# adaLN vectors of a two-layer diffusion backbone: the first partial sums are added on TensorE, block biases come one turn later, and layer 0's gate-2 blocks move to the output projection

## The chip, the cores and the metric

The kernel runs on one core of one Trainium2 chip. The metric is the device time of one execution in microseconds. Three runs of the kernel before took 2369.32 to 2370.25 us, their median is 2369.73 us.

## The reference

The program computes two layers of a diffusion backbone over 1024 latent tokens of 1024 features, in float32. Layer 0 mixes tokens by differential attention (8 heads, 256 context tokens in front of the latent ones), layer 1 by multi-scale centred pooling. Each layer ends in a dense SwiGLU FFN of width 2816. Every sub-layer is modulated by adaLN vectors and followed by a LayerNorm of `ALPHA * x + gate * y`. Cut to what matters here:

```python
def adaln_params(cond, w_mod, b_mod):
    m = jax.nn.silu(cond) @ w_mod + b_mod          # (1024,) @ (1024, 6144)
    return jnp.split(m, N_MOD, axis=-1)

for i in range(DEPTH):
    sh1, sc1, g1, sh2, sc2, g2 = adaln_params(c[:, None, :], w_mod[i], b_mod[i])
    csh1, csc1, cg1, csh2, csc2, cg2 = adaln_params(c_ctx, w_mod[i], b_mod[i])
    hx = modulate(x, sh1, sc1)                     # h * (1 + scale) + shift
    hc = modulate(h_ctx, csh1, csc1)
    y_lat = (attention of hx and hc) if i == 0 else multiscale_pool(hx, ...)
    x = layer_norm(ALPHA * x + g1 * y_lat, ln_g[i, 0], ln_b[i, 0])
    x = layer_norm(ALPHA * x + g2 * swiglu(modulate(x, sh2, sc2), ffn_w_in[i], ffn_w_out[i]),
                   ln_g[i, 1], ln_b[i, 1])
```

The adaLN vectors of a layer have 6144 entries: six vectors of 1024 features. The kernel makes them in blocks of 512 entries, so a layer has twelve blocks; blocks 0 to 3 are shift 1 and scale 1, and blocks 10 and 11 are gate 2. The context needs blocks 0 to 3 of layer 0 with its own condition.

## The kernel before, in words

**How a block is made.** An adaLN block is a product of a vector with a 1024 x 512 part of `w_mod`. It is done on VectorE: for each of eight row tiles of 128, a `[128, 512]` weight tile is multiplied with the condition's value of its partition and added to an accumulator `gacc` (L320 and L322 in the projections, L112 and L114 in `gemv_half`). Then TensorE adds up the 128 partitions: four matmuls with a matrix of ones on the other side write a PSUM tile `pg` (L298, L117; in float32, so the trace has two records for each matmul). Last, VectorE adds the bias (L299, L118). The weights come in four loads `gw` of 512 KB each.

**The first feature tiles.** Shift 1 and scale 1 of layer 0 are needed first, feature tile by feature tile, and have a layout of their own: `modulate_latents(k)` loads 1 MB (`wm`), makes two partial sums for the even and the odd row tiles (L233, L235; `acc[:, 0]` and `acc[:, 1]`), adds them (L237), sums over partitions on TensorE (`pm`, L240), adds the bias (L242, L243), and modulates the tile: ScalarE scales and rounds (L214, L215), GpSimd makes the low half (L216). TensorE's matmuls of the first three q and k products follow two tiles behind (L262).

**The products.** All large products are split into high and low halves (`fp32r`), so each is three matmuls. For each weight, ScalarE casts the high half and VectorE subtracts for the low half (L136 or L139 and L54 or L141 in the projections, L362 and L363 later).

**Turns.** During the projections, `turn()` is called once after each chain of 24 matmuls in `project_qk`, and before each in `project_v`. A turn takes one of the `turns` entries (a block's `gw` load, two row tiles), so a block takes four turns; the turn after that runs `sum_rows`: `pg` on TensorE and the bias. The first four blocks use the context's condition; when the fourth is summed, `context()` modulates the context tokens. `steps` gives the order of the products: the rest of q group 0, q groups 1 to 3, v group 0, k group 0's context tokens, k groups 1 to 3, v group 1. The loads of the next step's weights are written ahead of each step, through two raw buffers `wr`. There are two accumulators `gacc` and four `gw` buffers in this stage.

**Output projection and FFN.** `gemv1(b)` makes a block of layer 1. Blocks 0 and 1 are made in the output projection, behind feature tiles 1 and 4, and blocks 2 to 11 in layer 0's FFN, one behind each of its first ten groups. A group (of eleven) is: the products of w_in for two halves of 128 hidden features, done with seven products in place of eight (`p0` to `p6`, L641 to L643, 168 matmuls a group), then `beside(g)`, then the products with w_out (96 matmuls). In this stage the `gw` loads, the w_in loads (L693) and the w_out loads (L776) all share the four slots of one tag, `raw`, and there is one accumulator `gacc`.

**Order.** The compile step puts the instructions of each engine, and of each queue that issues DMAs, in a fixed order beforehand: an instruction that is ready by its own estimate goes, and among several ready ones the one that stands first in the program. The engines then run their lists in that order and wait with semaphores. A buffer that is used again waits for the readers of what it held.

Of the kernel before, what the change touches and what calls it, by code (L numbers as in the profile page):

```python
# [14 lines left out]
ALU = mybir.AluOpType  # L15
# [4 lines left out]
P = 128  # L20
D = 1024
KT = D // P
# [16 lines left out]
RAW, AOP, CT, QD = 4, 3, 5, 4  # L39
# [4 lines left out]
def backbone(ctx: ExitStack, tc: tile.TileContext, a: dict, out: bass.AP):  # L44
    nc = tc.nc
    V, S, G, PE, SP = nc.vector, nc.scalar, nc.gpsimd, nc.tensor, nc.sync
# [3 lines left out]
    def ctile(shape, name, dt=F32):  # L50
        return const.tile(shape, dt, name=name, tag=name)
# [9 lines left out]
    ones_f = ctile([P, P], "ones_f")  # L61
# [16 lines left out]
    def small_loads(pool):  # L78
        lamv = pool.tile([P, 4, HD], F32, name="lamv", tag="lamv")
        SP.dma_start(lng, a["lng"])  # L80
        SP.dma_start(lnb, a["lnb"])
        SP.dma_start(subg, a["subg"])
        SP.dma_start(pscale, a["pscale"])
        SP.dma_start(lamv, a["lam"].partition_broadcast(P))
        prod = pool.tile([P, 2, HD], F32, name="lamprod", tag="lamprod")
        V.tensor_tensor(prod[:, 0, :], lamv[:, 0, :], lamv[:, 1, :], ALU.mult)
        V.tensor_tensor(prod[:, 1, :], lamv[:, 2, :], lamv[:, 3, :], ALU.mult)
        ls = ctile([P, 2], "lamsum")
        V.reduce_sum(ls, prod, axis=AX.X)
        le = ctile([P, 2], "lamexp")  # L90
        S.activation(le, ls, AF.Exp)

        V.scalar_tensor_tensor(neglam, le[:, 1:2], -LAM_INIT, le[:, 0:1], ALU.add, ALU.subtract)
# [8 lines left out]
    def gemv_half(pool, psum, pstag, l, b, tags, bufs, wpool):  # L102

        acc = pool.tile([P, 512], F32, name="gacc", tag=tags[0], bufs=bufs[0])
        for k2 in range(KT // 2):
            wt = wpool.tile([P, 2, 512], F32, name="gw", tag=tags[1], bufs=bufs[1])
            SP.dma_start(wt, a["w_mod"][l, k2 * 2 * P:(k2 + 1) * 2 * P, b * 512:(b + 1) * 512]
                         .rearrange("(k p) f -> p k f", p=P))
            for i in range(2):
                k = 2 * k2 + i  # L110
                if k == 0:
                    V.tensor_scalar(acc, wt[:, i, :], sc_sb[:, 0, 0:1], None, ALU.mult)  # L112
                else:
                    V.scalar_tensor_tensor(acc, wt[:, i, :], sc_sb[:, k, 0:1], acc, ALU.mult, ALU.add)  # L114
        pg = psum.tile([P, 4, P], F32, name="pg", tag=pstag)
        for i in range(4):
            PE.matmul(pg[:, i, :], lhsT=acc[:, i * P:(i + 1) * P], rhs=ones_f, start=True, stop=True)  # L117
        V.tensor_tensor(modv[l][:, b * 4:(b + 1) * 4], pg[:, :, 0], bmod[:, l, b * 4:(b + 1) * 4], ALU.add)  # L118
# [4 lines left out]
    with ExitStack() as actx:  # L123
# [89 lines left out]
        def modulated(k, xk, sc, sh, t0, n):  # L213
            S.activation(xk, xk, AF.Identity, scale=sc, bias=sh)  # L214
            S.copy(hT_hi[:, k, t0:t0 + n], xk)  # L215
            G.tensor_tensor(hT_lo[:, k, t0:t0 + n], xk, hT_hi[:, k, t0:t0 + n].bitcast(F32), ALU.subtract)  # L216
# [5 lines left out]

        def modulate_latents(k):
            wm = pe.tile([P, KT, 256], F32, name="wm", tag="ot", bufs=2)
            SP.dma_start(wm, a["w_mod0"][k])
            xk = pa.tile([P, T], F32, name="xk", tag="xk", bufs=2)
            SP.dma_start(xk, a["xT"][k * P:(k + 1) * P, :])
            if k == 0:
                SP.dma_start(bmod, a["bmod"])
            acc = pa.tile([P, 2, 256], F32, name="acc", tag="gacc", bufs=2)  # L230
            for i in range(KT):
                if i < 2:
                    V.tensor_scalar(acc[:, i, :], wm[:, i, :], sc_sb[:, i, 0:1], None, ALU.mult)  # L233
                else:
                    V.scalar_tensor_tensor(acc[:, i % 2, :], wm[:, i, :], sc_sb[:, i, 0:1], acc[:, i % 2, :],  # L235
                                           ALU.mult, ALU.add)
            V.tensor_tensor(acc[:, 0, :], acc[:, 0, :], acc[:, 1, :], ALU.add)  # L237
            pm = psA.tile([P, 2, P], F32, name="pm", tag="mm")
            for i in range(2):
                PE.matmul(pm[:, i, :], lhsT=acc[:, 0, i * P:(i + 1) * P], rhs=ones_f, start=True, stop=True)  # L240
            sh, sc = modv[0][:, k:k + 1], modv[0][:, 8 + k:9 + k]
            V.tensor_tensor(sh, pm[:, 0, 0:1], bmod[:, 0, k:k + 1], ALU.add)  # L242
            V.scalar_tensor_tensor(sc, pm[:, 1, 0:1], 1.0, bmod[:, 0, 8 + k:9 + k], ALU.add, ALU.add)  # L243
            modulated(k, xk, sc, sh, CTX, T)
# [21 lines left out]
        cx = []  # L266

        def load_context():
            for k2 in range(2):
                cx.append(pa.tile([P, 4, CTX], F32, name="xk", tag="xk", bufs=2))  # L270
                SP.dma_start(cx[-1], a["ctxT"][k2 * 512:(k2 + 1) * 512, :].rearrange("(k p) t -> p k t", p=P))

        def context():
            V.tensor_scalar(modx[:, 8:16], modx[:, 8:16], 1.0, None, ALU.add)
            for k2 in range(2):
                xk = cx[k2]
                for k in range(4 * k2, 4 * k2 + 4):
                    modulated(k, xk[:, k % 4, :], modx[:, 8 + k:9 + k], modx[:, k:k + 1], 0, CTX)
# [1 line left out]


        GWL = 3
        turns = [(b, k2, 1) for b in range(4) for k2 in range(4)] + [(b, k2, 0) for b in range(4, 12) for k2 in range(4)]
        loaded, todo = [], []

        def load_rows():
            if len(loaded) < len(turns):
# [5 lines left out]
        def sum_rows():  # L293

            acc, b, j = todo.pop()
            pg = psA.tile([P, 4, P], F32, name="pg", tag="mm")
            for i in range(4):
                PE.matmul(pg[:, i, :], lhsT=acc[:, i * P:(i + 1) * P], rhs=ones_f, start=True, stop=True)  # L298
            V.tensor_tensor((modx if j else modv[0])[:, b * 4:(b + 1) * 4], pg[:, :, 0], bmod[:, 0, b * 4:(b + 1) * 4], ALU.add)  # L299

        done = [0]
        accs = [None]

        def turn():
            if todo:
                sum_rows()
                if done[0] == 12:
                    load_context()
                if done[0] == 16:
                    context()  # L310
            if done[0] == len(turns):
                return
            b, k2, j = turns[done[0]]
            load_rows()
            wt = loaded[done[0]]
            for i in range(2):
                k = 2 * k2 + i
                if k == 0:
                    accs[0] = pa.tile([P, 512], F32, name="gacc", tag="gacc", bufs=2)
                    V.tensor_scalar(accs[0], wt[:, i, :], sc_sb[:, 0, j:j + 1], None, ALU.mult)  # L320
                else:
                    V.scalar_tensor_tensor(accs[0], wt[:, i, :], sc_sb[:, k, j:j + 1], accs[0], ALU.mult, ALU.add)  # L322
            if k2 == 3:
                todo.append((accs[0], b, j))
            done[0] += 1
# [10 lines left out]
        for si, (kind, g, spans) in enumerate(steps):  # L336
            nxt = None
            if si + 1 < len(steps):
                nxt = w1 if si == 0 else weights(*steps[si + 1][0:2])
            if si == 1:  # L340
                small_loads(pa)
            if kind == 2:
                project_v(g, w)
            else:
                project_qk(kind, g, spans, w)
            w = nxt
# [9 lines left out]
    pwt = ctx.enter_context(tc.tile_pool(name="pwt", bufs=1, reuse_waits="tile"))  # L356
# [23 lines left out]
    with ExitStack() as bctx:  # L380
# [90 lines left out]
        for h in range(NH):  # L471
            g, hl = h // 2, h % 2
# [28 lines left out]
    pf = ctx.enter_context(tc.tile_pool(name="pf", bufs=1, reuse_waits="tile"))  # L501
    psM = ctx.enter_context(tc.tile_pool(name="psM", bufs=4, space=PSUM, reuse_waits="tile"))
    psL = ctx.enter_context(tc.tile_pool(name="psL", bufs=4, space=PSUM, reuse_waits="tile"))
# [131 lines left out]
    def gate_vector(l, gi, name):  # L635
        gt = ctile([P, KT], name)
        V.tensor_scalar(gt, modv[l][:, gi * 8:gi * 8 + 8], 1.0 / ALPHA, None, ALU.mult)
        return gt
# [11 lines left out]
        SP.dma_start(zT[:, k, :], a["xT"][k * P:(k + 1) * P, :])  # L650
    g1 = gate_vector(0, 2, "g1_0")
    M0 = ffn_mod(0)
    g2 = gate_vector(0, 5, "g2_0")
    def w_o(d, t0, n):
        wr = wo_raw.pop(0) if wo_raw else raw_o(d)
        p_ = bank()
# [6 lines left out]
        accumulate(d, slice(t0, t0 + n), p_[:, 0:n], g1)  # L663

    H = []
    def gemv1(b):
        gemv_half(pf, psL, "ln", 1, b, ("gacc", "raw"), (1, RAW), wpool=pwt)

    for d in range(KT):
        w_o(d, 0, 512)  # L670
        if d in (1, 4):
            gemv1(d // 4)
    rows = rows_of(0, 4)
    for d in range(KT):
        w_o(d, 512, 256)
# [183 lines left out]
            if t < 6:  # L859
                ln_rows(t, xr[t // 4][:, t % 4, :])  # L860

    ffn(0, g2, 0, M0, H, beside=lambda g: gemv1(g + 2) if g < 10 else None, after=ln_to_pool)

    A1 = one_plus(1, 1, "A1")
    V.tensor_tensor(A1, A1, lng[:, 1, :], ALU.mult)
# [52 lines left out]
    H = []  # L918
# [112 lines left out]
```

## Time and profile before

| | |
|---|---|
| median of 3 runs | 2369.73 us |
| the profiled execution | 2367.97 us, span 2366.2 us |
| TensorE busy | 2251.8 us, 95% of the span |
| VectorE busy | 1695.7 us, 72% |
| ScalarE, GpSimd busy | 932.7 us, 617.3 us |
| TensorE's granted clock over the span | 0.985 |

The page gives busy times of one execution. Matmuls are pipelined, so their records overlap: a matmul of 0.39 us starts every 0.23 us. An idle stretch stands in brackets behind the instruction that it precedes, with what ended it. The span has these stages: first feature tiles to 62 us, projections to 375 us, attention to 760 us, output projection to about 881 us, layer 0's FFN to about 1571 us, pooling, and layer 1's FFN to the end.

### The profile page before, as it was taken

The page shows a single profiled execution, that of the slowest core. Times are in us where ns is not written, and L with a number is a line of the kernel's source. Part 1 is how long each engine was busy: PE and PEld are TensorE (multiplying, and loading weights), DVE is VectorE, ACT ScalarE, POOL GpSimd, SP SyncE. Part 2 cuts the span into 40 slices and gives each one's busy share as a digit, 9 for nine tenths or more (in the row PEclk, how much of TensorE's full clock was granted, in tenths as well). Part 3 has the DMA queues.
Part 4 walks back from the last instruction along what each step waited for, and adds up shares of the span by engine and source line. Part 5 has one row for each costly group of instructions (what it writes and reads, how often), then busy time and mean ns, then how long its engine had stood idle before and what let it go on. Part 6 is the DMA issues. An engine that isn't in the chain of part 4 may idle for free.

```text
span 2366.2 us, 31051 instructions
## 1 busy us (share of the span) xinstructions
PE 2251.8 (95%) x11800; PEld 1916.2 (81%) x11800; DVE 1695.7 (72%) x2580; ACT 932.7 (39%) x1635; POOL 617.3 (26%) x618
## 2 busy tenths in 40 slices
PE   4979998999999997999999999998799999999997
PEld 3868887999998885888888888897588888888886
DVE  7763625999996689777777777757966666666678
ACT  3213115888876354222222222447422222222242
POOL 3432312444443043111111111103411111111122
PEclk9999999999999998999999999999899999999999
DMA  7866746333221532222222222212111111111121
GB/s 265 285 212 194 244 133 169 104 87 88 70 70 48 196 105 81 89 90 89 89 89 81 89 89 89 75 32 83 36 54 54 50 49 53 54 54 51 49 89 72
DMA packets 100918, 236.64 MB, mean 100 GB/s; under 512 B 9376, under 2 KB 27424, under 8 KB 99616
## 3 DMA queue, kind: packets, MB, share of 16 engines
q1 hardware_dynamic: 78688, 210.53, 27.5%
q10 hardware_dynamic: 22080, 24.12, 3.6%
q8 instruction: 93, 1.52, 0.3%
q14 instruction: 57, 0.47, 0.1%
HBM read 206.30 MB, written 28.31 MB: 99 GB/s over the span
## 4 chain that ended last, share of the span: by engine, by line
PE 84%; DVE 11%; DMA 1%; ACT 1%; issue 1%; POOL 1%; SPq 0%; DVEq 0%; ACTq 0%; POOLq 0%
PE mm L643 18%; PE mm L642 18%; PE mm L641 18%; PE s L400 6%; PE misc L431 6%; PE misc L424 3%; PE mm L171 2%; PE mm L170 2%; PE mm L169 2%; PE mm L160 1%; PE mm L161 1%; PE mm L159 1%; DVE aop L363 1%; DVE zT L646 1%; DVE acc L235 1%
## 5 line engine op out<-in xcount | busy, mean ns | idle before, releaser
L641 PE MATMUL mm<-H,aop 128*128 128x512 f32 x1232 | 484.1, 393 | 18.0 <-ACT aop L362 10.5
L643 PE MATMUL mm<-H,aop 128*128 128x512 f32 x1232 | 482.3, 392 | 6.7 <-DVE aop L363 6.7
L362 ACT CAST aop<-raw 128x512 fp32r<-128x512 f32 x392 | 241.8, 621 | 620.8 <-PE mm L643 578.5
L642 PE MATMUL mm<-H,aop 128*128 128x512 f32 x1232 | 483.2, 392 | 3.3 <-DVE H L363 3.3
L646 DVE SCALAR_TENSOR_TENSOR zT<-mm,g,zT 128x512 f32<-128x512 f32 (+1 forms) x400 | 276.9, 704 | 123.1 <-PE mm L643 121.1
L363 DVE TENSOR_TENSOR aop<-raw,aop 128x512 fp32r<-128x512 f32 x392 | 279.5, 716 | 111.3 <-ACT aop L362 110.2
L641 PEld LDWEIGHTS mm<-H,aop 128*128 128x128 f32 x1232 | 233.1, 189 | 68.8 <-ACT aop L362 13.2
L643 PEld LDWEIGHTS mm<-H,aop 128*128 128x128 f32 x1232 | 233.0, 189 | 57.6 <-DVE aop L363 9.6
L642 PEld LDWEIGHTS mm<-H,aop 128*128 128x128 f32 x1232 | 233.3, 189 | 52.3 <-DVE H L363 4.5
L642 PE MATMUL mm<-quad,aop 128*128 128x512 f32 x608 | 237.7, 391 | 1.5 <-DVE quad L363 1.5
L641 PE MATMUL mm<-quad,aop 128*128 128x512 f32 x608 | 237.6, 391 | 0.2 <-ACT aop L362 0.2
L643 PE MATMUL mm<-quad,aop 128*128 128x512 f32 x608 | 236.4, 390 | 0.0
L403 DVE TENSOR_REDUCE mx<-s 128x1 f32<-128x1280 f32 x128 | 190.7, 1490 | 38.7 <-PE s L400 33.8
L400 PE MATMUL s<-kk,qd 128*128 128x512 f32 (+1 forms) x768 | 181.9, 372 | 5.9 <-ACT e L406 3.1
L406 ACT ACTIVATE e<-s,mx 128x1280 f32<-128x1280 f32 x128 | 170.0, 1328 | 24.4 <-DVE mx L403 24.3
L718 POOL TENSOR_TENSOR raw<-s,raw 128x512 f32<-128x512 f32 x40 | 51.9, 1298 | 454.4 <-DVE aop L363 324.5
L400 PEld LDWEIGHTS s<-kk,qd 128*128 128x128 f32 x768 | 135.8, 190 | 30.4 <-ACT e L406 4.2
L431 PE MATMUL misc<-vv,at 128*128 128x128 f32 x1280 | 153.5, 275 | 0.6 <-ACT at L425 0.6
L409 POOL TENSOR_SCALAR e<-e,sm 128x1280 f32<-128x1280 f32 x64 | 88.2, 1378 | 250.7 <-DVE sm L407 247.4
L431 PEld LDWEIGHTS misc<-vv,at 128*128 128x128 f32 x1280 | 148.0, 192 | 0.8 <-ACT at L425 0.8
L642 PEld LDWEIGHTS mm<-quad,aop 128*128 128x128 f32 x608 | 114.2, 188 | 28.5 <-DVE quad L363 5.3
L641 PEld LDWEIGHTS mm<-quad,aop 128*128 128x128 f32 x608 | 114.2, 188 | 24.4 <-ACT aop L362 0.9
(176 smaller groups left out, 4081.3 us busy)
## 6 DMA issues: line engine op xcount, KB each, us to landing
gw<-in_w_mod SPq DMA_DIRECT2D x96, 512.0 KB, 4.5
raw<-in_w_in SPq DMA_DIRECT2D x88, 512.0 KB, 3.6
raw<-in_w_out SPq DMA_DIRECT2D x48, 512.0 KB, 3.4
qd<-q_d SPq DMA_DIRECT2D x64, 256.0 KB, 6.5
raw<-in_w_o SPq DMA_DIRECT2D x24, 512.0 KB, 3.7
kk<-k_d SPq DMA_DIRECT2D x8, 1280.0 KB, 6.3
wr<-in_w_qk SPq DMA_DIRECT2D x18, 512.0 KB, 5.5
wm<-in_w_mod SPq DMA_DIRECT2D x8, 1024.0 KB, 7.3
```

Of the source, the lines that this page charges most:

```text
L362: S.copy(hi, src)
L363: (eng or V).tensor_tensor(lo, src, hi.bitcast(F32), ALU.subtract)
L400: PE.matmul(ps[:, lo_:hi_], lhsT=self.qd[:, m, s, q0:q0 + P], rhs=self.kk[:, m, lo_:hi_], start=(s == 0), stop=(s == 1))
L403: V.tensor_reduce(mx, ps[:, 0:TA], axis=AX.X, op=ALU.max, negate=True)
L406: S.activation(e, ps[:, 0:TA], AF.Exp, bias=mx, accum_out=sm)
L409: G.tensor_scalar(e, e, sm, 1.0, ALU.mult, ALU.mult)
L424: PE.transpose(pt[:, j, :], self.e[0][:, (kb + j) * P:(kb + j + 1) * P], ident)
L431: PE.matmul(av, lhsT=self.at[:, kb, :], rhs=self.vv[:, kb, :], start=(kb == 0), stop=(kb == NTT - 1))
L641: PE.matmul(p_, lhsT=wh, rhs=xh, start=first, stop=False)
L642: PE.matmul(p_, lhsT=wh, rhs=xl, start=False, stop=False)
L643: PE.matmul(p_, lhsT=wl, rhs=xh, start=False, stop=last)
L646: V.scalar_tensor_tensor(zT[:, d, cs], p_, gate[:, d:d + 1], zT[:, d, cs], ALU.mult, ALU.add)
```

## The change

The first `wm` load is issued in four parts. The two partial sums of a first feature tile are no longer added on VectorE: TensorE runs two matmuls for each half of `pm` and adds the partials in PSUM. In the projections, `sum_rows` only issues `pg`, and the bias is added by a new function `vector()` at the next turn, which also starts `context()`. Two turns are left empty at the beginning of step 3 (q group 3), and the list of turns ends with block 9 rather than 11. Blocks 10 and 11 of layer 0 are made in the output projection, where blocks 0 and 1 of layer 1 were made, and the gate-2 vector is built behind them. The twelve blocks of layer 1 are all made in layer 0's FFN: none behind group 0, two behind each of groups 1, 2 and 3, and one behind each of groups 4 to 9.

```diff
         def modulate_latents(k):
             wm = pe.tile([P, KT, 256], F32, name="wm", tag="ot", bufs=2)
-            SP.dma_start(wm, a["w_mod0"][k])
+            if k == 0:
+                for i in range(0, KT, 2):
+                    SP.dma_start(wm[:, i:i + 2], a["w_mod0"][k, :, i:i + 2])
+            else:
+                SP.dma_start(wm, a["w_mod0"][k])
...
-            V.tensor_tensor(acc[:, 0, :], acc[:, 0, :], acc[:, 1, :], ALU.add)
             pm = psA.tile([P, 2, P], F32, name="pm", tag="mm")
             for i in range(2):
-                PE.matmul(pm[:, i, :], lhsT=acc[:, 0, i * P:(i + 1) * P], rhs=ones_f, start=True, stop=True)
+                for j in range(2):
+                    PE.matmul(pm[:, i, :], lhsT=acc[:, j, i * P:(i + 1) * P], rhs=ones_f, start=(j == 0), stop=(j == 1))
...
-        turns = [(b, k2, 1) for b in range(4) for k2 in range(4)] + [(b, k2, 0) for b in range(4, 12) for k2 in range(4)]
-        loaded, todo = [], []
+        turns = [(b, k2, 1) for b in range(4) for k2 in range(4)] + [(b, k2, 0) for b in range(4, 10) for k2 in range(4)]
+        loaded, todo, summed = [], [], []
...
                 PE.matmul(pg[:, i, :], lhsT=acc[:, i * P:(i + 1) * P], rhs=ones_f, start=True, stop=True)
+            summed.append((pg, b, j))
+
+        def vector():
+
+            pg, b, j = summed.pop()
             V.tensor_tensor((modx if j else modv[0])[:, b * 4:(b + 1) * 4], pg[:, :, 0], bmod[:, 0, b * 4:(b + 1) * 4], ALU.add)
+            if j and b == 3:
+                context()
...
+        quiet = [0]
+
         def turn():
+            if quiet[0]:
+                quiet[0] -= 1
+                return
+            if summed:
+                vector()
             if todo:
                 sum_rows()
-                if done[0] == 12:
-                    load_context()
-                if done[0] == 16:
-                    context()
+            if done[0] == 12 and not cx:
+                load_context()
...
             if si == 1:
                 small_loads(pa)
+
+            if si == 3:
+                quiet[0] = 2
...
     M0 = ffn_mod(0)
-    g2 = gate_vector(0, 5, "g2_0")
...
-    def gemv1(b):
-        gemv_half(pf, psL, "ln", 1, b, ("gacc", "raw"), (1, RAW), wpool=pwt)
+    def gemv(l, b):
+        gemv_half(pf, psL, "ln", l, b, ("gacc", "raw"), (1, RAW), wpool=pwt)

     for d in range(KT):
         w_o(d, 0, 512)
         if d in (1, 4):
-            gemv1(d // 4)
+            gemv(0, 10 + d // 4)
+    g2 = gate_vector(0, 5, "g2_0")
...
-    ffn(0, g2, 0, M0, H, beside=lambda g: gemv1(g + 2) if g < 10 else None, after=ln_to_pool)
+    def beside(g):
+        for b in {0: (), 1: (0, 1), 2: (2, 3), 3: (4, 5)}.get(g, (g + 2,) if g < 10 else ()):
+            gemv(1, b)
+
+    ffn(0, g2, 0, M0, H, beside=beside, after=ln_to_pool)
```

## Rows read from the trace of the kernel before

**Rows 1.** The page, part 1: busy time, share of the span, instructions.
```profile
PE 2251.8 (95%) x11800; PEld 1916.2 (81%) x11800; DVE 1695.7 (72%) x2580; ACT 932.7 (39%) x1635; POOL 617.3 (26%) x618
```
**Rows 2.** TensorE's waits, 27 to 380 us: total us, times, longest.
```profile
PE mm L160 <- DVE wl L54: 8.0, 1, 8.0
PE pm L240 <- DVE acc L237: 7.4, 5, 1.5
PE mm L171 <- DVE wl L141: 3.3, 1, 3.3
...
PE mm L159 <- DVE modx L299: 1.7, 1, 1.7
```
**Rows 3.** Stretches: length, busy PE, PEld, DVE, ACT, POOL; PEclk, DMA, GB/s.
```profile
62.00:122.00 60.00, 60.00 (x271) 49.83 (x270) 40.27 (x55) 14.55 (x19) 30.48 (x21) 1.00 0.80 265
...
173.00:176.50 3.50, 3.43 (x9) 2.71 (x10) 3.50 (x5) 0.00 (x0) 1.28 (x1) 0.54 0.78 263
...
996.40:1057.15 60.75, 60.75 (x275) 50.46 (x274) 45.06 (x68) 16.97 (x29) 11.64 (x9) 1.00 0.27 87
```
**Rows 4.** Timeline of TensorE, 173 to 177 us: start, us, what, idle before.
```profile
173.07 0.80 PE L160 MATMUL mm<-wl,hT_hi 128*128 128x512 f32 x1 [7.98 <-DVE wl L54]
...
176.22 0.39 PE L159 MATMUL mm<-wh,hT_hi 128*128 128x512 f32 x1
```
**Rows 5.** Timeline of the first feature tiles, 7 to 24 us.
```profile
7.15 2.46 DVE L235 SCALAR_TENSOR_TENSOR acc<-wm,sc_sb,acc 128x256 f32<-128x256 f32 x6
...
10.12 1.22 PE L240 MATMUL pm<-ones_f,acc 128*128 128x128 f32 x4 [10.12 <-DVE acc L237]
...
20.11 4.55 DVE L235 SCALAR_TENSOR_TENSOR acc<-wm,sc_sb,acc 128x256 f32<-128x256 f32 x6
...
20.96 2.62 POOL L216 TENSOR_TENSOR hT_lo<-xk,hT_hi 128x1024 fp32r<-128x1024 f32 x1 [4.25 <-ACT hT_hi L215]
```
**Rows 6.** Timeline of VectorE at the sum of tile 5's partials.
```profile
45.29 2.48 DVE L237 TENSOR_TENSOR acc<-acc 128x256 f32<-128x256 f32 x1
```
**Rows 7.** L216, 38 to 66 us: ns min/median/max, first and last start.
```profile
L216 POOL TENSOR_TENSOR hT_lo<-xk,hT_hi x5: 2397/2638/2640, 38.4 to 64.4; 128x1024 fp32r<-128x1024 f32 x5
```
**Rows 8.** Timeline of VectorE in the projections.
```profile
122.88 0.16 DVE L299 TENSOR_TENSOR modx<-pg,bmod 128x4 f32<-128x4 f32 x1 [8.10 <-PE pg L298]
122.96 0.48 DVE L320 TENSOR_SCALAR gacc<-gw,sc_sb 128x512 f32<-128x512 f32 x1
...
150.64 0.16 DVE L299 TENSOR_TENSOR modx<-pg,bmod 128x4 f32<-128x4 f32 x1 [11.51 <-PE pg L298]
```
**Rows 9.** TensorE's waits in layer 0's FFN, 935 to 1490 us.
```profile
PE pg L117 <- DVE gacc L114: 1.0, 1, 1.0
```
**Rows 10.** SyncE's queue, 930 to 1490 us: its waits for w_out's slots.
```profile
SPq L776 <- DVE gacc L114: 53.6, 19, 3.1
```
**Rows 11.** Timeline of FFN group 1: w_out loads, pg, first output matmul, bias.
```profile
978.71 3.90 SPq L776 DMA_DIRECT2D raw<-in_w_out  x2
...
995.57 1.05 PE L117 MATMUL pg<-ones_f,gacc 128*128 128x128 f32 x8
996.37 0.48 PE L641 MATMUL mm<-quad,aop 128*128 128x512 f32 x1
...
997.71 0.15 DVE L118 TENSOR_TENSOR modv<-pg,bmod 128x4 f32<-128x4 f32 x1
```
**Rows 12.** The w_out loads (L776), 930 to 1490 us: issue to landing.
```profile
DMA to landing us min/median/max: 3.2/3.5/4.3
```
**Rows 13.** Timeline of VectorE in the output projection, second block.
```profile
783.33 0.49 DVE L112 TENSOR_SCALAR gacc<-gw,sc_sb 128x512 f32<-128x512 f32 x1
...
785.61 4.74 DVE L114 SCALAR_TENSOR_TENSOR gacc<-gw,sc_sb,gacc 128x512 f32<-128x512 f32 x6 [0.24 <-DMA gw<-in_w_mod]
...
790.72 0.69 DVE L363 TENSOR_TENSOR aop<-raw,aop 128x512 fp32r<-128x512 f32 x1 [0.36 <-ACT aop L362]
```
**Rows 14.** Timeline of ScalarE at the context tokens' casts.
```profile
208.98 0.71 ACT L215 CAST hT_hi<-xk 128x256 fp32r<-128x256 f32 x2 [16.21 <-issue]
```

## Prediction

> **What bounds the kernel now.** I read the page first: TensorE is busy for 95% of the span [rows 1], so time is lost or won where TensorE stands idle. Its waits, asked for by stretch, come next. Between 27 and 380 us four of them lie where the change works [rows 2]: five waits for the sum of the two adaLN partials (L237), 7.4 us in all, then 3.3, 1.7 and 8.0 us in the projections, where a weight's low half (L141, L54) or a block's bias (L299) is late on VectorE. From 62 to 122 us and in the FFN groups of layer 0 TensorE has no gap [rows 3]: there, a new wait on TensorE is a loss of its full length. A matmul of 512 columns takes 0.228 us (the 60 us less 16 bias records of 0.11, over 255), a chain of 24 takes 5.5.
>
> A wait also costs clock. After the 8.0 us wait the granted clock over 173 to 176.5 was 0.54, so mostly the 1.2 GHz level [rows 3], and seven matmuls took from 173.07 to 176.22 [rows 4], 3.15 us for 1.6 of work. I add 1.6 us to every wait of 3 us or more and nothing to shorter ones, which is a choice.
>
> **The first feature tiles (L225 to L243).** The first wm load comes in four parts. Today the eight sums start when the whole tile has landed. With parts, six of them lie under the load, four L235 and two L233, at 0.4 and 0.3 each [rows 5] 2.2 us; I take 1.9, as the parts cost issue time. The sum L237 (0.43) goes; pm takes eight records in place of four, which at the spacing there (four in 1.22 [rows 5]) adds 1.2. So the first bias is about 1.1 earlier. It doesn't last: VectorE operations with both inputs in SBUF don't run while GpSimd's L216 runs. Six L235 took 2.46 us alone and 4.55 beside L216 [rows 5]; L237 took 2.48 beside it [rows 6]. Ending sooner, tile 0's L216 falls on the last sums of tile 1, and tile 1's bias is back near its old time.
>
> For tiles 3 to 7 one period is 6.5 us (five L216 from 38.4 to 64.4 [rows 7]), of which 2.9 is VectorE's sums and 2.6 L216 with L237 stuck behind it. Without L237 the sums of one tile slip through before L216 starts (a period of about 4.5), and those of the next begin behind it and are cut by the following one (about 7.4). The mean is 5.9, and over these tiles the last pm comes about 2.1 us sooner. Five pm of four more records cost 2.3 us of TensorE, which lie in what is left of its idle time. TensorE will also have fewer matmuls behind it when the last pm comes, so I take 1.5 us won, between 0 and 4.
>
> The Trainium skill, on its page "SBUF — State Buffer", section "Who interferes with whom", says that a VectorE instruction with two SBUF inputs and a GpSimd instruction that reads SBUF exclude each other, and that whichever issues first holds the port to its end. By that rule the trace agrees, and removing one blocked instruction hands the block to the next; without such a lock all five waits would go, 7.4 less 2.3, so 5.1 us.
>
> **The bias one turn later (L299).** In VectorE's order L299 is followed at once by L320 of the block after next [rows 8], which needs the accumulator that the same pg matmuls free (there are two buffers). VectorE would wait for pg at that place with or without the bias. I take 0, within 2 us either way.
>
> **The two quiet turns and the shorter list.** Two turns are skipped at the start of the fourth q step, so block 2's pg stands two chains (11 us) later, and with it L299, L320 and seven sums. Today VectorE sits 11.51 us before L299 at 150.64 [rows 8], with the first v weight's low half queued behind, and the chain of weight buffers (two raw ones) then delivers the later halves at 173, the wait of 8.0 for L54 [rows 2]. Without it they can be made from about 146 on, and the fourth by 158, before TensorE needs it near 160. So 1.7 + 8.0 + 1.6 of clock, 11.3 us, can go; I take 9.8, as something of it will come back. The wait of 3.3 (and 1.6 of clock) stands behind block 1's pg, ahead of the quiet turns; I leave it. Ends: 0, and 16.2 (all three). The eight turns that leave hide under TensorE now; their leaving is worth 0.
>
> **Gate-2 blocks in the output projection.** gemv(0, 10) and gemv(0, 11) take the places of gemv1(0) and gemv1(1): same loads (eight of 512 KB on SyncE's queue), same sums, same pg. 0.
>
> **The FFN of layer 0.** Group 0 loses its block and the 1.0 us wait for it [rows 9]: −1.0. Groups 1, 2, 3 get two blocks each instead of one, and this is the costly part. One block fits today: its loads take raw slots early, its pg runs at its program place, behind the 168 product matmuls, and w_out is there by then. But every w_out load waits for a slot that the block's sums free (L776 for L114, 19 times) [rows 10]. With two blocks, the second's four gw loads take all four raw slots ahead of w_out, since the queue keeps the program's order; and they can't be used up, since there is one accumulator, which is free only after the first block's pg, at the end of the products. So behind pg stands, in series: the bias from 997.71 to 997.87, L112 and L114 (0.49, and 0.79 as six of them in 4.74 [rows 11, 13], so 1.3), the w_out load, 3.5 us to landing [rows 12], and ScalarE's cast, 0.6. The first output matmul, today at 996.37 [rows 11], would start at 1003.3.
>
> The third matmul also needs VectorE's low half. In the output projection, where two blocks already follow each other, that L363 ran at 790.72, after the last of the second block's sums [rows 13]. Here: eight sums, 6.0 us from 997.87, to 1003.9; L363 0.7, to 1004.6; and up to 1.8 for product results that VectorE still owes. That is 8.2 to 10.0 after 996.37; two matmuls (0.45) and the second pg (0.9) run in the hole, so 6.9 to 8.7 are lost, and 1.6 of clock: 8.5 to 10.3. I take 9.5; the ends are 6.5 (L363 goes first) and 12 (another load ahead in the queue). Three groups: +28.5, between 19.5 and 36. Nothing hides it: TensorE is busy for 60.75 of 60.75 us in a group [rows 3], and the next group's products need raw slots that come after w_out.
>
> **Sum.** −1.5 + 0 − 9.8 + 0 − 1.0 + 28.5 = +16.2 us. The profiled execution took 2367.97 (span 2366.2): 2384.2 for it, and the median of the runs, 2369.73, lies 1.8 above, so 2386. This forecast's own range is 2373 to 2399.
>
> **Rivals.** (1) The w_out wait doesn't appear: the first block's pg slips in among the products (its last sums were done by 982.6, when the second w_out load was issued, 13 us before pg [rows 11]), the second block is summed under the products, and w_out lands in time. It decides if TensorE meets pg some 10 us before the products end. Against it: today's pg stands exactly behind them in every group from 1 on, and only group 0's ever waited [rows 9, 11]. Then the gains alone stand: 2369.7 − 12.3 = 2357, faster. (2) The FFN waits come and the projections win nothing: the context tokens' modulation begins three turns later, and ScalarE stood 16.21 us in front of its casts today [rows 14]. Such a wait in front of the first context chain eats the 9.8, and up to 8 more: 2396 to 2404, middle 2399. That the bias move does nothing is in the sum already.
>
> **Chances.** Forecast 0.61, rival 1 0.22, rival 2 0.17. A measurement tells 0.2%, 4.7 us, from no change. Faster by more: most of rival 1 and a sliver of the forecast, 0.24. Within: 0.08. Slower: 0.68. The range runs from rival 1 to rival 2, 2357 to 2401.
>
> **What would show it.** Right: in groups 1 to 3 a wait of 6 to 9 us on TensorE at its first output matmuls, for L362 or L363 of w_out, with the L776 load issued 1 to 4 us after pg, and a granted clock near half behind it; pm waits of mixed length in place of five of 1.5; no wait of 8 us near 170. Wrong: pg of the first block among the products; groups of 61.6 us; or new waits before the context chain near 200 us.

## The result and the profile after

The changed kernel takes 2389.48 us (median of 5 runs, 2388.46 to 2392.0), the kernel before 2369.73 (5 runs beside it). The ratio is 1.0086, 95% interval 1.0071 to 1.0101, so 17 to 24 us slower. The forecast was 2386, slower, with the doubled FFN groups as the cause. The profiled execution has a span of 2387.7 us.

TensorE's busy time rose by 14 us against [rows 1] (page, part 1). Some 6 of them belong to `pm`, which has 32 records more; and the granted clock over the span fell from 0.985 to 0.981. So part of the loss is clock, not waiting.

```profile
PE 2265.8 (95%) x11832; PEld 1928.1 (81%) x11832; DVE 1688.2 (71%) x2572; ACT 933.1 (39%) x1635; POOL 616.1 (26%) x618
```

Where the time went is read from the same landmarks in both traces, in us from the span's start (first matmul of attention, first w_in product, first w_out matmul of groups 0, 1 and 4, end):

| | attention | FFN | group 0 | group 1 | group 4 | end |
|---|---|---|---|---|---|---|
| before | 375.1 | 874.2 | 933.3 | 996.4 | 1178.6 | 2366.2 |
| changed | 367.9 | 865.7 | 925.0 | 992.5 | 1200.0 | 2387.7 |
| difference | -7.2 | -8.5 | -8.3 | -3.9 | +21.4 | +21.5 |

So 8 us are won up to the FFN, and from group 0's to group 4's w_out the changed kernel takes 274.9 us in place of 245.3: +29.7. Behind that nothing changes. A group boundary of one profile is good to about 2 us: kernels with the same median differ by so much at the start of attention (below).

**The FFN wait.** TensorE's waits from 935 to 1490 us (total us, times, longest); in [rows 9] the one wait there was 1.0 for pg:

```profile
PE mm L660 <- ACT aop L381: 19.7, 3, 6.7
```

The chain of waits through group 1 (start, us, what) shows what the first w_out matmul (L660) waited for:

```profile
984.83 0.24 PE mm L662
...
985.09 0.69 DVE ct L771
985.78 0.60 DVE quad L382
986.38 0.60 DVE ct L772
986.98 0.07 DVE modv L118
987.05 0.40 DVE gacc L112
...
987.48 0.76 DVE gacc L114
...
988.26 3.44 DMA raw<-in_w_out
...
991.80 0.63 ACT aop L381
...
992.47 0.79 PE mm L660
...
994.12 1.99 PE pg L117 x8
```

The last product ends, VectorE works off what it owes and adds the first block's bias (L118); only then may the second block's first two products run (L112, L114), which frees the slot that the w_out load (988.26) waits for; it lands after 3.44 us, is cast, and TensorE goes on. SyncE's queue shows the same wait from its side (930 to 1300 us; the longest in [rows 10] was 3.1):

```profile
SPq L795 <- DVE gacc L114: 43.6, 10, 9.0
```

This answers to [rows 11 to 13] step for step: the load left 3.4 us after pg began (984.89), and the matmul came 7.6 us after pg where the forecast had 7.7.

Granted clock behind the waits of the changed kernel (stretch: length, busy PE, PEld, DVE, ACT, POOL; PEclk, DMA, GB/s), to be held against [rows 3]:

```profile
130.40:133.40 3.00, 2.93 (x8) 2.33 (x9) 1.18 (x3) 1.70 (x3) 3.00 (x3) 0.63 0.96 343
163.70:166.70 3.00, 2.95 (x13) 2.45 (x14) 1.20 (x2) 0.72 (x1) 1.29 (x1) 1.00 0.98 362
178.80:181.80 3.00, 2.98 (x7) 2.40 (x8) 2.89 (x4) 0.00 (x0) 1.22 (x1) 0.53 0.84 264
992.40:998.35 5.95, 5.88 (x18) 4.57 (x19) 3.72 (x7) 1.16 (x3) 0.00 (x0) 0.52 0.68 226
```

Behind the FFN wait TensorE ran 5.95 us at 0.52, the 1.2 GHz level: 5.95 x 0.48 = 2.9 us lost. A doubled group costs 6.5 of wait, 0.8 for the second pg (as long as the eight records from 995.57 to 996.37 in [rows 11]) and 2.9 of clock, 10.2 in all. The landmarks give 10.7: +29.7, and 2.4 more that group 0 gives back (below), over three. The half microsecond between the two is not accounted for.

**The projections.** TensorE's waits, 27 to 380 us, answering to [rows 2]:

```profile
PE mm L160 <- DVE wl L54: 5.3, 2, 3.0
PE pm L244 <- DVE acc L239: 3.3, 2, 1.9
PE mm L171 <- DVE wl L141: 3.3, 1, 3.3
```

The waits of 8.0 and 1.7 became 3.05 (at 163.75) and 2.30 (at 178.81); five waits for pm became two. VectorE's timeline shows why something came back:

```profile
142.18 1.22 DVE L54 TENSOR_TENSOR wl<-wr,wh 128x1024 fp32r<-128x1024 f32 x1
...
154.61 0.16 DVE L308 TENSOR_TENSOR modx<-pg,bmod 128x4 f32<-128x4 f32 x1 [10.62 <-PE pg L302]
...
155.20 5.48 DVE L338 SCALAR_TENSOR_TENSOR gacc<-gw,sc_sb,gacc 128x512 f32<-128x512 f32 x7
...
161.79 1.91 DVE L54 TENSOR_TENSOR wl<-wr,wh 128x1024 fp32r<-128x1024 f32 x1
...
169.74 0.16 DVE L308 TENSOR_TENSOR modx<-pg,bmod 128x4 f32<-128x4 f32 x1 [4.84 <-PE pg L302]
...
177.54 2.35 DVE L54 TENSOR_TENSOR wl<-wr,wh 128x1024 fp32r<-128x1024 f32 x2
```

The first low half of the v weights (L54) now runs at 142, ahead of block 2's bias, where it stood behind it before. The second stands behind that bias and eight sums, the third and fourth behind block 3's. The second also holds one of the two raw buffers while it stands there: the fourth weight's load leaves SyncE's queue only at 163.73, and ScalarE casts it at 169.89.

### The profile page after: what moved, and what is told of

It is laid out like the page before. It is cut to its first block, busy times and chain, and to the rows that moved or that the text cites. A ratio compares the mean times of both kernels' runs of the same rounds, so it can differ in the third digit from the quotient of the medians.

```text
span 2387.7 us, 31124 instructions
## 1 busy us (share of the span) xinstructions
PE 2265.8 (95%) x11832; PEld 1928.1 (81%) x11832; DVE 1688.2 (71%) x2572; ACT 933.1 (39%) x1635; POOL 616.1 (26%) x618
## 4 chain that ended last, share of the span: by engine, by line
PE 84%; DVE 10%; DMA 2%; ACT 1%; issue 1%; POOL 1%; SPq 0%; DVEq 0%; ACTq 0%; POOLq 0%
PE mm L661 18%; PE mm L662 18%; PE mm L660 18%; PE s L419 6%; PE misc L450 6%; PE misc L443 3%; PE mm L171 3%; PE mm L169 3%; PE mm L170 3%; PE mm L160 1%; PE mm L161 1%; PE mm L159 1%; DVE aop L382 1%; DVE quad L382 1%; DVE zT L665 1%
## 5 line engine op out<-in xcount | busy, mean ns | idle before, releaser
L660 PE MATMUL mm<-H,aop 128*128 128x512 f32 x1232 | 484.4, 393 | 18.0 <-ACT aop L381 10.5
L665 DVE SCALAR_TENSOR_TENSOR zT<-mm,g,zT 128x512 f32<-128x512 f32 (+1 forms) x400 | 277.2, 704 | 133.1 <-PE mm L662 131.2
L382 DVE TENSOR_TENSOR aop<-raw,aop 128x512 fp32r<-128x512 f32 x392 | 280.5, 718 | 119.9 <-ACT aop L381 118.8
L660 PEld LDWEIGHTS mm<-H,aop 128*128 128x128 f32 x1232 | 233.6, 190 | 69.1 <-ACT aop L381 13.2
L660 PE MATMUL mm<-quad,aop 128*128 128x512 f32 x608 | 240.4, 395 | 20.0 <-ACT aop L381 19.7
L661 PE MATMUL mm<-quad,aop 128*128 128x512 f32 x608 | 239.9, 395 | 2.1 <-DVE quad L382 2.0
L662 PE MATMUL mm<-quad,aop 128*128 128x512 f32 x608 | 238.8, 393 | 0.0
L422 DVE TENSOR_REDUCE mx<-s 128x1 f32<-128x1280 f32 x128 | 190.8, 1490 | 39.0 <-PE s L419 34.0
L660 PEld LDWEIGHTS mm<-quad,aop 128*128 128x128 f32 x608 | 115.7, 190 | 44.8 <-ACT aop L381 20.2
```

Of the source, the lines that this page charges most:

```text
L382: (eng or V).tensor_tensor(lo, src, hi.bitcast(F32), ALU.subtract)
L422: V.tensor_reduce(mx, ps[:, 0:TA], axis=AX.X, op=ALU.max, negate=True)
L660: PE.matmul(p_, lhsT=wh, rhs=xh, start=first, stop=False)
L661: PE.matmul(p_, lhsT=wh, rhs=xl, start=False, stop=False)
L662: PE.matmul(p_, lhsT=wl, rhs=xh, start=False, stop=last)
L665: V.scalar_tensor_tensor(zT[:, d, cs], p_, gate[:, d:d + 1], zT[:, d, cs], ALU.mult, ALU.add)
```

## The experiments

All were timed beside the kernel before (4 to 11 runs each; the kernel before had medians of 2368.2 to 2369.2). Differences in us are the ratio less 1, times 2368.

### The FFN: which part of the doubling costs

**The blocks alone**, on the kernel before:

```diff
-turns = ... for b in range(4, 12) ...
+turns = ... for b in range(4, 10) ...
-            gemv1(d // 4)
+            gemv(0, 10 + d // 4)
-ffn(..., beside=lambda g: gemv1(g + 2) if g < 10 else None, ...)
+ffn(..., beside=beside, ...)        # none, two, two, two, then one
```

> The kernel before with only the blocks moved (gate 2 of layer 0 to the output projection, none behind group 0, two behind groups 1, 2 and 3); first feature tiles, biases and turns as before, apart from the eight turns that leave. Theory: a doubled group costs 10.7 us (in the changed kernel three periods of 71.3 to 71.5 against 60.75), group 0 gives back 1.0, so +31: 2401, with TensorE waits of 6 to 7 us at the first output matmul of groups 1 to 3. Rival: the doubled groups cost less without the earlier start of the attention, or the shorter list of turns wins something by itself: under 2396.

Measured: 2394.96, ratio 1.0112 (1.0098 to 1.0126), +26.5. TensorE's waits, 980 to 1260 us:

```profile
PE mm L641 <- ACT aop L362: 19.9, 3, 6.7
```

The waits are those of the changed kernel, so they don't depend on the earlier start. From group 0 to group 4 the FFN takes 274.3 us, +29.0. The expectation's +31 was 4.5 too high. Three groups a little cheaper (10.5 each) make 0.7 of it. Another 1.4 is what group 0 gives back: 2.4, not 1.0 (from its first w_out matmul to the next pg is 62.2 us in the kernel before, 59.8 in the changed one), as I had left out the pg itself. The rest is attention, which starts 2.5 earlier in this profile. The rival, that the shorter list of turns wins something by itself, was to show as a time under 2396, and the time is 1 us under it; but 2.5 is hardly more than the scatter of one profile, so this stays open.

**w_out loaded ahead of the second block**, on the changed kernel:

```diff
+            two = beside is not None and g in (1, 2, 3)
+            if two:
+                wrs = [out_raw(g, hf) for hf in range(2)]
+                gemv(1, 2 * g - 1)
...
-                    wr = out_raw(g, hf)
+                    wr = wrs[hf] if two else out_raw(g, hf)
...
-        for b in {0: (), 1: (0, 1), 2: (2, 3), 3: (4, 5)}.get(g, (g + 2,) if g < 10 else ()):
+        for b in {0: (), 1: (0,), 2: (2,), 3: (4,)}.get(g, (g + 2,) if g < 10 else ()):
```

> The changed kernel, in groups 1 to 3 with both w_out loads issued ahead of the second block's four loads; still two blocks in these groups and one accumulator. Theory (order in the queue: the second block's loads hold the slots that w_out needs): the wait of 6.5 and the 3.0 of low clock behind it go, the second pg's 0.85 stays; the next group's w_in loads now stand behind the block and may cost up to 3 each: 2361 to 2370. Rival (VectorE has too much to do behind the products, 6 us of sums more): 2380 or more.

Measured: 2366.36, ratio 0.999 (0.9981 to 0.9999). SyncE's queue in group 1 (start, length of the stretch, what, how many):

```profile
954.67 11.29 SPq L107 DMA_DIRECT2D gw<-in_w_mod  x4
968.84 3.91 SPq L795 DMA_DIRECT2D raw<-in_w_out  x2
974.21 16.00 SPq L107 DMA_DIRECT2D gw<-in_w_mod  x4
992.49 10.26 SPq L712 DMA_DIRECT2D raw<-in_w_in  x4
```

The w_out loads go at 969, the second block's behind them, and from 980 to 1260 us only 1.5 us of TensorE waits are left. The second block is summed between the accumulations of w_out, its pg comes at 998.2. A doubled group still costs 1.6 to 1.9 (62.3, 62.7 and 62.4 from one first w_out matmul to the next, in place of 60.75), of which 0.8 is its pg. Same sums, same loads, same accumulator; the edit moves two loads ahead in one queue, what the compile step makes of the other lists follows from that, and 23 us are won.

**A second accumulator**, on the changed kernel, queue order untouched:

```diff
...
-            gemv(1, b)
+            gemv(1, b, *(("s1", 2) if g in (1, 2, 3) and b % 2 else ()))
```

> The changed kernel, in groups 1 to 3 with an accumulator of its own for the second block (a buffer of the tag s1, which is idle at that time); queue order as it was. Theory (the single accumulator is what holds the second block's loads in the slots): its sums run under the products, w_out loads leave before pg, and the wait falls from 6.5 to 0 to 3: 2360 to 2373. Rival (the four slots are the limit: eight loads pass through the two that w_in leaves, and w_out is late with or without the second accumulator): waits of 5 us or more stay, 2382 to 2390.

Measured: 2369.75, ratio 1.0008 (0.9999 to 1.0016). SyncE's queue in group 1, and then TensorE's waits from 980 to 1260 us:

```profile
954.44 21.09 SPq L107 DMA_DIRECT2D gw<-in_w_mod  x8
977.71 4.72 SPq L795 DMA_DIRECT2D raw<-in_w_out  x2
```
```profile
PE mm L660 <- DVE zT L665: 5.1, 3, 1.9
```

All eight loads pass before the products end, and w_out leaves at 977.7, 8 us ahead of pg (985.5). So the four slots were not the limit by themselves: they were held because the accumulator was. The two cures are two ends of the same chain. What is left is a wait of 1.5 to 1.9 us a group for VectorE, whose additions of the w_out results (L665) start only when the rest of its work, 16 sums among it, is done; the clock behind these waits stayed at 1.00, and the groups cost 1.8 to 3.1 more than 60.75.

**One block a group, the two that are over in the last pass of the output projection**, on the changed kernel:

```diff
+        if d in (5, 6):
+            gemv(1, d - 5)
...
     def beside(g):
-        for b in {0: (), 1: (0, 1), ...}.get(...):
-            gemv(1, b)
+        if g < 10:
+            gemv(1, g + 2)
```

> The changed kernel with one block behind each of groups 0 to 9 again and the two that are over in the last pass of the output projection (behind d = 5 and 6). Theory: the three stalls go (3 x 10.7), group 0 takes its 1.0 back: 2389.5 - 32 + 1 = 2358, about 11 below the kernel before. Rival: the output projection's last pass has no room for two more blocks (its weight loads use the same four slots) and waits 3 to 8 us there: 2361 to 2366. If the stalls have another cause than the second block, 2380 or more.

A miss: 2379.57, ratio 1.0045 (1.0031 to 1.0059), +10.7. The FFN is as before (245.0 from group 0 to 4), but the output projection (from its first product to the first w_in product) takes 132.0 us in place of 112.8. SyncE's queue there, then the clock behind two of its waits (columns as above):

```profile
846.12 13.64 SPq L107 DMA_DIRECT2D gw<-in_w_mod  x4
862.86 0.34 SPq L392 DMA_DIRECT2D raw<-in_w_o  x1
864.70 4.60 SPq L107 DMA_DIRECT2D gw<-in_w_mod  x4
871.91 0.34 SPq L392 DMA_DIRECT2D raw<-in_w_o  x1
```
```profile
866.90:872.90 6.00, 5.99 (x27) 5.70 (x28) 4.27 (x9) 0.48 (x1) 0.00 (x0) 0.53 0.88 293
877.30:883.30 6.00, 5.92 (x28) 5.70 (x29) 4.29 (x8) 1.16 (x3) 0.00 (x0) 0.55 0.78 238
```

It is the FFN's stall again in another place: each w_o load stands behind four gw loads. TensorE waits 1.2, 6.1 and 3.7 us, and 2.8 and 2.7 go to the clock. My rival had the place right and the price far too low.

### First tiles, bias and quiet turns, each by itself on the kernel before

**First feature tiles alone** (wm in parts, the partials added on TensorE; the change's first two hunks).

> The kernel before with the changes of the first feature tiles alone: wm in four parts, the partial sums added on TensorE. By the prediction's step -1.5 us (0 to 4 won). Theory now: in the changed kernel the last pm comes 3.3 us sooner (58.0 in place of 61.3) and the first products end behind it, so up to -3.3: 2365 to 2368. Rival: what is won there is given back at the next late weight half in the projections, whose chain of loads and casts does not start sooner: 2368 to 2369, waits of 2 to 3 us more near 130 or 170.

Measured: 2368.52, ratio 1.0 (0.9991 to 1.0009). In its trace the last pm comes 3.4 us sooner (57.9 against 61.3), the wait near 130 1.4 sooner, and attention starts 1.3 sooner. This agrees with the step's -1.5, but the timing can't tell it from nothing.

**Two quiet turns alone** (`quiet[0] = 2` at step 3).

> The kernel before with only the two turns left empty at the start of step 3; the bias stays in its turn, the list of turns is whole. By the prediction's step the 8.0 and 1.7 us waits go and with them 1.6 of clock: -9.8, so 2358. Theory now: VectorE's sums of the next block stand in front of another low half, and the wait comes back in two parts (3.05 and 2.30 in the changed kernel): -4 to -6, so 2362 to 2364.

Measured: 2365.38, ratio 0.9988 (0.9979 to 0.9997), -2.8. TensorE's waits, 27 to 380 us:

```profile
PE mm L160 <- DVE wl L54: 5.4, 2, 3.0
PE mm L171 <- DVE wl L141: 3.3, 1, 3.3
```

The same two waits as in the changed kernel take the place of 8.0 and 1.7. The forecast's -9.8 took both as gone; of my theory after the result, -4 to -6, the interval (-0.7 to -5.0) reaches only the near end.

**The bias one turn later alone** (`summed`, `vector()`).

> The kernel before with only the bias added one turn later (and the context's modulation with it). By the prediction's step 0 within 2 us, because the first product of the block after next waits for the same pg matmuls: 2366 to 2370. Rival: with the bias out of VectorE's way the low half that stands behind it comes up to 11 us sooner, and the waits near 162 and 173 shrink as they do in the changed kernel: 2360 to 2364.

Measured: 2367.92, ratio 0.9999 (0.999 to 1.0008): nothing. Its trace still has waits of 1.7, 7.6 and 3.3 us; the bias runs behind pg at once (pg at 147.7, bias at 148.8), so the fixed order put it there although it is written one turn later. In this profile attention starts at 373.0, 2.1 before that of the kernel before, at the same median: the scatter spoken of above.

**Three accumulators** in the first tiles and the projections, on the kernel with w_out first (the products for lambda are made in place, which frees the room):

```diff
...
-accs[0] = pa.tile([P, 512], F32, name="gacc", tag="gacc", bufs=2)
+accs[0] = pa.tile([P, 512], F32, name="gacc", tag="gacc", bufs=3)
```

> The changed kernel with w_out loaded first (as in the run with both w_out loads ahead of the second block), and three accumulators in place of two in the first feature tiles and the projections (lambda's products are made in place to free the room). Theory (VectorE's sums wait for the pg that frees the accumulator, and the low halves behind them wait along): with a third one a block's sums do not wait for pg, the low halves come in time, and the waits of 3.3, 3.1 and 2.3 us shrink or go: 2366.4 - 5 to 10 = 2356 to 2361. Rival (the order of VectorE's list or the weight loads hold the low halves): 2364 to 2368, waits of the same length.

Measured: 2365.71, ratio 0.9987 (0.9978 to 0.9995), 0.7 below the kernel that it is built on, which these runs can't tell from nothing. The waits, 27 to 380 us:

```profile
PE mm L159 <- DVE wl L54: 5.4, 2, 3.0
PE mm L170 <- DVE wl L140: 3.3, 1, 3.3
```

The theory falls: in the projections VectorE doesn't wait for the accumulator. It waits for pg because the bias, the next instruction of its list, reads pg.

### What else stands behind the bias

**Low halves of v group 0 on GpSimd**, on the kernel with w_out first, then on the kernel before, then the first of these without the quiet turns:

```diff
-                sub_hi(wl, wr, wh)
+                if low is None:
+                    sub_hi(wl, wr, wh)
+                else:                      # low=G for v group 0
+                    low.tensor_tensor(wl, wr, wh.bitcast(F32), ALU.subtract)
```

> The changed kernel with w_out loaded first, and the low halves of v group 0's weights made on GpSimd in place of VectorE. Theory (a low half is ready for VectorE by 146, but stands in its list behind a bias that waits for pg, and behind eight sums): out of that list, the TensorE waits near 164 and 179 (3.05 and 2.3) go, with 1 to 3 us of clock; the one near 130 (a q weight, still on VectorE) stays: 2366.4 - 6 to 8 = 2358 to 2360. Rival (the loads through two raw buffers, or ScalarE's casts behind its own DMA issues, are what is late): the waits stay or move, 2365 to 2368.

> The kernel before with only the low halves of v group 0's weights made on GpSimd; no quiet turns, no late bias. Theory (same place in VectorE's list): the waits near 163 and 173 (1.7 and 8.0) and the clock behind them shrink by 6 to 10, without any change to the turns: 2358 to 2362. Rival (the loads or the casts are late): 2366 to 2369.

> As the run with the low halves on GpSimd on top of the changed kernel, but without the two empty turns (the bias still one turn later). Theory: with the low halves out of VectorE's list the quiet turns have nothing left to do, so the same time as with them, within 3 us: 2357 to 2362. Rival: they still win by themselves, as VectorE's rope products also stand behind the bias: 3 to 5 slower than with them.

Measured: 2364.67 (0.9981, 0.9972 to 0.999), 2373.75 (1.0023, 1.0014 to 1.0033) and 2372.19 (1.0017, 1.0008 to 1.0026). My theory that the low halves' place in VectorE's list was the cause falls. In the first of these runs one wait of 4.5 us stands in place of 3.05 and 2.30, and the time differs from that of the kernel that it is built on (2366.36) by less than the intervals can tell apart. On the kernel before it makes things 5.4 us worse. GpSimd's timeline of that run:

```profile
170.50 1.27 POOL L195 TENSOR_TENSOR ta<-ta,tb 128x512 f32<-128x512 f32 x1 [11.14 <-DVE ta L193]
171.73 2.34 POOL L140 TENSOR_TENSOR wl<-wr,wh 128x1024 fp32r<-128x1024 f32 x1
```

This low half (L140), the second, has its cast weight at 157.6, but now stands in GpSimd's list behind the rope sum L195, which waits for VectorE's rope product L193, which stands behind the bias and the sums of two blocks (152.8 to 169.8). The chain goes on to ScalarE, whose weight casts stand behind its own q_d stores of the rope result (its cast at 170.61 sat 13.03 us behind one). Moving one link leaves it whole. The quiet turns, which move the bias itself, are worth 7.5 us here (2372.19 against 2364.67), more than the 2.8 that they are worth on the kernel before and than the 3 to 5 that the rival gave them: without them TensorE waits 2.7 and 7.1 us there, with them 4.5.

The Trainium skill, on its page "Perfetto Trace Analysis", section "Optimizing Scalar/DVE Operations", warns that moving work from VectorE to GpSimd may not help, since they share a port. That VectorE pays for it shows in the same run: L323 beside L140 took 1.99 us, where the same operation takes 0.48 alone. That nothing is won comes from the order of the lists, as the 11.14 us show: TensorE's waits there are 2.7 and 7.1 us, in sum as long as the 1.7 and 8.0 of the kernel before. What the trace shows as lost is clock, behind both waits (columns as above):

```profile
163.20:166.50 3.30, 3.30 (x8) 2.62 (x9) 2.62 (x5) 0.00 (x0) 0.00 (x0) 0.50 0.86 290
174.10:180.10 6.00, 5.98 (x14) 4.71 (x15) 0.00 (x0) 1.75 (x3) 4.15 (x3) 0.50 0.77 255
```

That costs 1.65 and 3.0 us. In the kernel before the clock was 1.00 behind the first of the two waits (162.7 to 165.7) and 0.54 over 3.5 us behind the second [rows 3], 1.6. The difference is some 3 us, and by 3.0 attention starts later in this run (378.1). The other 2.4 of the 5.4 I can't place.

**Quiet turns one step earlier**, on the first of these:

```diff
-            if si == 3:
-                quiet[0] = 2
+            quiet[0] += {2: 2, 3: 1}.get(si, 0)
```

> As the run with the low halves on GpSimd on top of the changed kernel, but two turns are left empty at the start of step 2 and one at the start of step 3, in place of two at step 3. In VectorE's list the rope products and the two low halves of the q weights now stand ahead of block 1's bias, where they stood behind its eight sums. Theory (whatever stands behind a bias in VectorE's list waits for pg): the wait of 3.28 near 130 goes, with 1 to 2 of clock: 2364.7 - 3 to 6 = 2359 to 2362. Rival (the wait moves on to the next bias, or the context tokens come one turn too late for their first chain): 2364 or more, with a wait of 3 or more between 130 and 230.

Measured: 2362.77, ratio 0.9976 (0.9967 to 0.9985), 3.6 to 7.8 us below the kernel before: the fastest version here, ahead of both kernels. VectorE's timeline (in brackets the idle time before, and what ended it):

```profile
118.14 1.21 DVE L144 SCALAR_TENSOR_TENSOR wl<-wr,wh 128x1024 fp32r<-128x1024 f32 x1
...
123.70 1.69 DVE L144 SCALAR_TENSOR_TENSOR wl<-wr,wh 128x1024 fp32r<-128x1024 f32 x1
...
138.29 0.16 DVE L311 TENSOR_TENSOR modx<-pg,bmod 128x4 f32<-128x4 f32 x1 [11.06 <-PE pg L305]
```

Both q low halves run ahead of block 1's bias, and the wait of 3.3 near 130 is gone. One wait of more than 0.3 us is left in the projections, for a low half of v:

```profile
PE mm L163 <- POOL wl L140: 5.9, 1, 5.9
```

VectorE still stands idle for 11 us in front of a bias, but what TensorE needs next is already made. The wait for the low half was 4.5 in the run without the earlier turns, so part of the gain came back there, and the time lies between the theory's 2362 and the rival's 2364. Its time against the run without the earlier turns (2364.67) differs by less than the two intervals can tell apart.

## Why the prediction came out right, step by step

- **Doubled FFN groups (+28.5).** Right in mechanism and nearly in size: 10.7 a group in place of 9.5. The signs named for it came: the wait is at the first w_out matmul, the load leaves 3.4 us after pg, and the clock behind it is near half. The wait was 6.5, a little under the 6.9 to 8.7 of the working, as the low half goes ahead of the last sum (L382 at 992.57); the prediction kept that case for its lower end. But that end, 6.5 for the whole of a group, was too low, as two terms were off the other way: the second pg didn't run in the hole but behind it (0.8), and the clock cost 2.9, not 1.6. The runs with w_out first and with two accumulators show that both links of the chain (held slots, single accumulator) are needed.
- **Group 0 (-1.0).** -2.4 in the trace. The term counted the wait and forgot the pg.
- **Quiet turns (-9.8).** The term most mis-sized: -2.8 alone (0.7 to 5.0). The first low half came 10 us sooner, as said. The step failed where it says that "the fourth by 158": the third and fourth were made from 177.5. Each later block's bias stops VectorE in the same way, and the block's eight sums stand behind it; the second low half, kept back so, held the raw buffer in which the fourth weight was to land (its load left at 163.73).
- **Bias one turn later (0).** Right, for another reason than given. The prediction named the accumulator; a third one changes no wait of the projections.
- **First tiles (-1.5).** The trace agrees (1.3 to 1.4 sooner), the timing can't tell. The mechanism was seen: six L239 take 2.46 us in one tile and 4.56 in the next, in turn, and L216 starts 4.8 and 6.5 us apart (37.13, 41.91, 48.41) where the prediction had 4.5 and 7.4. VectorE's timeline of the changed kernel:

```profile
35.08 2.46 DVE L239 SCALAR_TENSOR_TENSOR acc<-wm,sc_sb,acc 128x256 f32<-128x256 f32 x6
...
40.11 4.56 DVE L239 SCALAR_TENSOR_TENSOR acc<-wm,sc_sb,acc 128x256 f32<-128x256 f32 x6
...
46.36 2.46 DVE L239 SCALAR_TENSOR_TENSOR acc<-wm,sc_sb,acc 128x256 f32<-128x256 f32 x6
```

- **Gate 2 in the output projection (0).** The stage took 112.8 us in the changed kernel and 115.3 in the run with the blocks alone, 114.2 before: nothing that one profile can tell.
- **The sum.** +16.2 was forecast, about +20 measured (17 to 24). First tiles and projections won 4.1 us less than said in the trace of the changed kernel (7.2 before attention, 11.3 forecast), and the FFN cost 2.2 more; 1.3 more were won in the output projection, which I can't place. The two errors go the same way, so the forecast was not saved by one hiding the other. The times agree: between the changed kernel and the run with the blocks alone lie about 6 us, where 11.3 were forecast. The three parts by themselves gave 0, -2.8 and 0, less than 6 in sum, but each within 2; they were not run together without the FFN's change.
- **Rivals.** The first (no wait for w_out) is out: pg stood behind the products in all three groups. The second is out, too: no wait appeared in front of the context chain (TensorE has none between 182 and 365 us). The projections did win less than said, but for the reason above. The numbers given for it don't fit each other: 2396 to 2404 has its middle at 2400, not 2399, and the whole range ends at 2401.

## What to carry to other kernels

Before a second helper task goes into a stage, follow its loads through the queue that they share with the main work: if they can only be used up after an event at the stage's end, they hold the buffers in front of the main work's next load, whatever bandwidth is free; issue the main load first. An instruction that reads another engine's late result stops everything written behind it on its engine, and through the engines that this one feeds; move the instruction, not one of its victims. Price a new wait on TensorE by the granted clock behind it, too, and as a range, since it is not the same in every run (next section).

## What the runs showed of the hardware

The clock behind a wait doesn't follow from its length alone. In the changed kernel TensorE was granted 0.52 for 6 us behind a wait of 6.5 us in the FFN, 0.63 over the 3 us behind 3.3 us (at 130.4) and 0.53 behind 2.3 (at 178.8), but 1.00 behind 3.05 (at 163.7). Ahead of all four TensorE had run without a gap for at least 12.7 us, so these rows don't say what made the difference. One and the same wait shows it more plainly. The 3.28 us near 130 stand in the run with the bias alone and in the run with the quiet turns alone, and in both TensorE had run without a gap since 61 us. Behind the wait the clock was, in this order (columns as above):

```profile
131.30:134.30 3.00, 3.00 (x13) 2.50 (x14) 1.16 (x2) 1.58 (x2) 3.00 (x3) 1.00 1.06 401
131.40:137.40 6.00, 5.97 (x14) 4.72 (x15) 3.64 (x5) 1.95 (x3) 4.83 (x4) 0.50 0.92 329
```

So the same wait cost nothing in the one trace and 3.0 us of clock in the other. My rule, a price for waits from 3 us on and none below, was wrong on both sides of its bound, and the clock alone can shift a stage by some 3 us from one profile to the next. And a bias written one turn later ran at the same place, 1.1 us behind its pg.
